# A fixed order of TensorE's work in the expert loop: first product, next tokens, turn, selection, second product

## The chip, the cores and the metric

The kernel runs on one NeuronCore of a Trainium2 chip. Its time is the device time of one execution in microseconds (us); before and after are compared by the median of several executions. One execution of each kernel is also profiled, and the rows below come from that one.

## The reference

Two transformer blocks over 512 tokens of width 1024, in float32. The first block has a mixer (a gated delta rule beside sliding-window attention) and then a mixture of experts; the second block has two feed-forward layers around another mixer. The change lies in the mixture of experts:

```python
out = jnp.zeros(t.shape, jnp.float32)
for e in range(N_EXPERTS):                               # 32 experts
    hid = jax.nn.silu(t @ w_gate[e]) * (t @ w_up[e])     # 1024 -> 2 x 256
    out = out + combine[:, e:e + 1] * (hid @ w_down[e])  # 256 -> 1024
```

`combine` is zero but for the two experts that a token has chosen, so each expert needs only its own tokens: 32 of the 512 on the mean.

## The kernel before, in words

The kernel is one program for the five engines, written with a library that records the operations, places their buffers and then puts each engine's instructions in an order of its own, by readiness and priority under its model of times; data dependences become semaphores. So the order of the source isn't the order on an engine.

The experts are worked through in `moe` in 8 quads of 4 experts. A quad's first pass takes at most 32 tokens of each expert: the array's 128 columns are split in four strips of 32, and four matmuls, one per expert, run side by side. In quad q:

- `expert1` (line 1257), the **first product**: 8 steps of the inner dimension times 4 experts, 32 matmuls of 512 columns on the gate and up weights. The profile records a float32 matmul as two, so 64 records. ScalarE and VectorE then make the gated units `mth` from it (lines 1247 to 1249: tanh, scalar-tensor-tensor, product).
- `xpose` (line 1228): 8 **token transposes** of `xg`, the gathered tokens of quad q+1; `feed` scales them into `xgT`, VectorE the even and ScalarE the odd ones (lines 1218, 1216). `xgT` has one buffer, which the running first product still reads.
- `turn` (line 1266): two transposes of `mth`, copied by ScalarE into `hT` (line 1268).
- `expert2` (line 1289), the **second product**: 16 matmuls of 512 columns on the down weights; ScalarE scales the result into `ys` (line 1290), GpSimd scatters it.
- `gather(q + 2)` with `select` (line 1173): the **selection**, 32 small matmuls as recorded, of 3 columns, gives the token numbers of the quad after the next; GpSimd then gathers these tokens.
- `more`, per expert: under a condition read from the data (line 1347) a **wide pass** over up to 128 more tokens. In these data one expert of each quad takes it. Behind each `more`, six weight tiles of 512 KB are asked for (`load`, line 1031, by SyncE's queue).
- `ahead(q + 1)` (lines 1340, 1342): under conditions again, the selection for the next wide pass (line 1203).

What stands under a condition can't move out of it, nor the rest in. So between `ahead(q)` and `more` the library is free in the order of the first product, token transposes, turn, second product and selection; that is the stretch that the change touches. The weights have 31 buffers: 24 tiles of a quad and 7 of the next.

Of the kernel before, what the change touches and what calls it, by code (L numbers as in the profile page):

```python
# [21 lines left out]
KT = 8  # L22
# [182 lines left out]
class Net:  # L205
# [804 lines left out]
    def moe(self):  # L1010


        nc, v, s, g_, pe = self.nc, self.nc.vector, self.nc.scalar, self.nc.gpsimd, self.nc.tensor
        A, tc, mp = self.A, self.tc, self.mp
        mm, ident, ones, mod = pe.matmul, self.ident, self.ones, self.mod

        NQ = NE // 4
        first, wide = 32, 128

        def ex(q, c):  # L1020

            return 8 * c + q
# [10 lines left out]
        def piece(w, k):  # L1033

            return w[k // 2][:, k % 2 * S:k % 2 * S + S]
# [17 lines left out]
        for i in range(4):  # L1053
            for hf in range(2):
                pt = self.pst([P, S], "mm")
# [6 lines left out]
        def sm(shape, tag):  # L1062
            return self.t(mp, shape, "r_" + tag)
# [79 lines left out]
        val = sm([P, 4, NE, 3], "val")  # L1143
# [19 lines left out]
        def select(q):  # L1163

            oh = self.t(mp, [P, 4, 4, first], "oh")
            for i in range(4):
                v.tensor_tensor(oh[:, i], iota[:, :first].unsqueeze(1).to_broadcast([P, 4, first]),
                                rank[:, i, q::8].unsqueeze(2).to_broadcast([P, 4, first]), ALU.is_equal)
            pv = self.pst([P, 3], "mm")
            for i in range(4):  # L1170
                for c in range(4):
                    cs = slice(32 * c, 32 * c + 32)
                    mm(pv[cs, :], oh[:, i, c, :], val[:, i, ex(q, c), :], start=i == 0, stop=i == 3, tile_position=(0, 32 * c))
            if q < NQ - 1:
                idx = self.t(mp, [P, 1], "idy", U32, bufs=4)
                v.tensor_scalar_add(idx, pv[:, 2:3], BIG - 1.0)
            else:
                idx = self.t(mp, [P, 1], "idx")
                v.tensor_scalar_add(idx, pv[:, 0:1], BIG)
            wv = self.t(mp, [P, 1], "wv", bufs=4)  # L1180
            v.tensor_copy(wv, pv[:, 1:2])
            return oh, idx, wv, pv

        def fetch_tokens(xg, idu):
            g_.indirect_dma_start(out=xg, out_offset=None, in_=h2d, in_offset=bass.IndirectOffsetOnAxis(ap=idu, axis=0),
                                  bounds_check=S - 1, oob_is_err=False)

        def gather(q):

            _, idx, wv, pv = select(q)  # L1190
            idu = self.t(mp, [P, 1], "idu", U32, bufs=4)
            v.tensor_scalar_add(idu, pv[:, 0:1], BIG - 1.0)
            fetch_tokens(xg, idu[:, 0:1])
            return xg, idx, wv
# [25 lines left out]
        def xtiles():  # L1220
            return [self.t(mp, [P, 4, P], f"xgT{hf}") for hf in range(2)]

        def xpose(xg, xTs=None):
            xTs = xTs or xtiles()
            for hf in range(2):
                pt = self.pst([P, 4, P], "mm")
                for k in range(4):
                    pe.transpose(pt[:, k, :], xg[:, (4 * hf + k) * P:(4 * hf + k + 1) * P], ident)
                feed(xTs, hf, pt)
            return xTs  # L1230
# [14 lines left out]
        def glu(th, gate, up):  # L1245

            s.activation(th, gate, AF.Tanh, scale=0.5)
            v.scalar_tensor_tensor(th, th, 1.0, gate, op0=ALU.add, op1=ALU.mult)
            v.tensor_mul(th, th, up)

        def expert1(q, xT):
            ps = self.pst([P, 2, 2, P], "mm")
            ws = [[wt[ex(q, c), j] for j in range(4)] for c in range(4)]
            for k in range(KT):
                for c in range(4):
                    cs = slice(32 * c, 32 * c + 32)
                    mm(ps[cs].rearrange("p a b c -> p (a b c)"), xT[k // 4][:, k % 4, cs], piece(ws[c], k),  # L1257
                       start=k == 0, stop=k == KT - 1, tile_position=(0, 32 * c))
            th = self.t(mp, [P, 2, P], "mth")
            glu(th, ps[:, :, 0, :], ps[:, :, 1, :])  # L1260
            return th

        def turn(th):
            pt = self.pst([P, 2, P], "mm")
            for k in range(2):
                pe.transpose(pt[:, k, :], th[:, k, :], ident)
            hT = self.t(mp, [P, 2, P], "hT")
            s.copy(hT, pt)
            return hT
# [5 lines left out]
        def expert2(q, hT, idx, wv):  # L1275

            late = q == NQ - 1
            ys = yt[:1]
            if late:
                ys = [self.t(mp, [P, D], f"ys{i}", F32R) for i in range(2)]  # L1280
                ys.append(self.t(self.tp, [P, S], "sq", F32R))
                v.tensor_scalar(ys[-1], tokens, idx, None, op0=ALU.is_equal)
            for n in range(2):
                py = self.pst([P, S], "mm")
                ns = slice(n * S, (n + 1) * S)
                for k in range(2):
                    for c in range(4):
                        cs = slice(32 * c, 32 * c + 32)
                        mm(py[cs, :], hT[:, k, cs], wt[ex(q, c), 4 + k][:, ns], start=k == 0, stop=k == 1, tile_position=(0, 32 * c))  # L1289
                s.activation(ys[0][:, ns], py, AF.Copy, scale=wv)  # L1290
                if late:
                    v.scalar_tensor_tensor(ys[1][:, ns], py, wv, ys[0][:, ns], op0=ALU.mult, op1=ALU.subtract)
            if not late:
                scatter(ys[0], idx[:, 0:1])
            return ys
# [41 lines left out]
        def ahead(q):  # L1337

            for h in range(2):
                with tc.If(rvs[NE + 8 * h + q] > first):  # L1340
                    for c in (2 * h, 2 * h + 1):
                        with tc.If(rvs[ex(q, c)] > first):
                            gather_wide(ex(q, c), 1)
# [37 lines left out]
        gat = {0: select(0)}  # L1381
        xt = pick(gat[0][0])
        gat[1] = gather(1)
        count(0)
        for q in range(NQ):
            last = q == NQ - 1
            th = expert1(q, xt)
            if q == 0:
                ahead(0)
            if not last:  # L1390
                xt = xpose(gat[q + 1][0])
                count(q + 1)
            hT = turn(th)
            if not last:
                expert2(q, hT, *gat[q][1:3])
                if q + 2 < NQ:
                    gat[q + 2] = gather(q + 2)
            for c in range(4):
                more(ex(q, c))
                load(6)  # L1400
            if not last:
                ahead(q + 1)
# [518 lines left out]
```

## Time and profile before

| what | value |
|---|---|
| median of 3 runs | 2187.48 us (2181.98 to 2188.98) |
| profiled execution | 2189.56 us, span of the trace 2187.7 us |
| TensorE busy | 2028.8 us, 93% of the span |
| first products, line 1257 | 512 records, 77.7 us |
| second products, line 1289 | 256 records, 49.5 us |
| expert loop, first product of quad 0 to the scatter of quad 7 | 497.3 to 804.4 us |

The trace gives for each instruction its start and length, and for the idle time of an engine before it what ended it. A view by stretches gives busy time per engine and the TensorE clock granted, as a share of 2.4 GHz: 1.00 is the full clock, 0.50 is 1.2 GHz.

### The profile page before, as it was taken

Reading aid. Unit: us, or ns where it says so; the run is one execution under the profiler, and the core shown is the slowest. Engines: PE = TensorE matmul, PEld = TensorE weight load, DVE = VectorE, ACT = ScalarE, POOL = GpSimd, SP = SyncE. Lnnn points to the kernel's source line nnn. Section 1 sums busy time; section 2 is a strip of 40 time slices with the busy share of each in tenths; the row PEclk is TensorE's granted clock in tenths of the full one; section 3 lists DMA queues with packets and bytes.
Section 4 is the critical chain, followed back from the end, with each engine's and each line's share of the span. In section 5 each row is a group of like instructions: output and inputs, shape, how many; then the busy total and the mean of one; then the engine's idle time right before and its main releaser. Section 6 shows DMA issues by size and latency. Waiting matters only on the chain.

```text
span 2187.7 us, 32948 instructions
## 1 busy us (share of the span) xinstructions
PE 2028.8 (93%) x13074; PEld 1566.6 (72%) x13074; DVE 1045.1 (48%) x1947; ACT 703.9 (32%) x1173; POOL 186.2 (9%) x208
## 2 busy tenths in 40 slices
PE   5999999788888878999999899999999999999996
PEld 3677767554343438888888788888878888888886
DVE  4663564742111127552354764745564447542454
ACT  3432343121221214322233342534452343322231
POOL 3020002001001012000002300000000031000002
PEclk9999999888898989999999999999999999999998
DMA  7343315057999854233232232323222322233321
GB/s 266 107 127 104 101 55 177 30 181 306 383 347 352 333 216 142 97 93 99 100 97 94 72 92 70 123 63 113 64 98 93 109 78 81 98 90 98 106 87 40
DMA packets 106470, 294.40 MB, mean 135 GB/s; under 512 B 16087, under 2 KB 27351, under 8 KB 106284
## 3 DMA queue, kind: packets, MB, share of 16 engines
q1 hardware_dynamic: 99676, 275.98, 36.7%
q0 software_dynamic: 6032, 13.85, 1.9%
q8 instruction: 117, 1.92, 0.4%
q10 hardware_dynamic: 576, 2.10, 0.2%
q14 instruction: 69, 0.57, 0.1%
HBM read 283.53 MB, written 18.13 MB: 138 GB/s over the span
## 4 chain that ended last, share of the span: by engine, by line
PE 56%; DVE 3%; POOL 1%; ACT 1%; issue 1%; DMA 0%; POOLq 0%; SPq 0%; ACTq 0%; DVEq 0%
PE mm L274 18%; PE mm L273 18%; PE mm L275 17%; DVE xl L1535 1%; PE sm L1633 1%; POOL x L1487 1%; PE mm L1661 1%; DVE cy L1486 1%; PE mm L1658 0%; DVE wl L257 0%; PE sm L1648 0%; PE sm L1787 0%; POOL ss L339 0%; ACT wh L256 0%; DVE rs_a L297 0%
## 5 line engine op out<-in xcount | busy, mean ns | idle before, releaser
L273 PE MATMUL mm<-xh,wh 128*128 128x512 f32 (+1 forms) x1584 | 615.3, 391 | 5.6 <-ACT xh L1534 4.1
L274 PE MATMUL mm<-xl,wh 128*128 128x512 f32 (+1 forms) x1584 | 606.0, 383 | 4.9 <-DVE xl L1535 4.9
L275 PE MATMUL mm<-xh,wl 128*128 128x512 f32 (+1 forms) x1584 | 603.4, 382 | 0.5 <-DVE wl L257 0.5
L256 ACT ACTIVATE wh<-wraw 128x1024 fp32r<-128x1024 f32 (+3 forms) x282 | 274.2, 974 | 747.6 <-PE mm L274 663.6
L257 DVE TENSOR_TENSOR wl<-wraw,wh 128x1024 fp32r<-128x1024 f32 (+3 forms) x282 | 314.6, 1116 | 192.1 <-ACT wh L256 190.4
L273 PEld LDWEIGHTS mm<-xh,wh 128*128 128x128 f32 x1584 | 301.9, 192 | 71.8 <-issue 8.3
L274 PEld LDWEIGHTS mm<-xl,wh 128*128 128x128 f32 x1584 | 303.2, 191 | 60.8 <-DVE xl L1535 6.6
L275 PEld LDWEIGHTS mm<-xh,wl 128*128 128x128 f32 x1584 | 302.3, 191 | 57.1 <-issue 1.2
L273 PE MATMUL mm<-hh,wh 128*128 128x512 f32 (+1 forms) x416 | 148.5, 357 | 0.0
L275 PE MATMUL mm<-hh,wl 128*128 128x512 f32 (+1 forms) x416 | 148.3, 357 | 0.0
L274 PE MATMUL mm<-hl,wh 128*128 128x512 f32 (+1 forms) x416 | 148.2, 356 | 0.0
L339 POOL TENSOR_TENSOR ss<-ss,sq 128x256 f32<-128x256 f32 (+1 forms) x69 | 65.7, 952 | 915.9 <-ACT sq L338 913.4
L275 PEld LDWEIGHTS mm<-hh,wl 128*128 128x128 f32 x416 | 78.6, 189 | 11.3
L273 PEld LDWEIGHTS mm<-hh,wh 128*128 128x128 f32 x416 | 78.6, 189 | 11.3
L274 PEld LDWEIGHTS mm<-hl,wh 128*128 128x128 f32 x416 | 78.6, 189 | 11.2
L1257 PE MATMUL mm<-wmoe,xgT 128*32 128x512 f32 x512 | 77.7, 630 | 6.8 <-PEq L1340 4.9
L1595 DVE TENSOR_TENSOR sq<-mm,rsb 128x512 f32<-128x512 f32 x44 | 30.4, 691 | 104.0 <-PE mm L275 103.8
L1590 DVE TENSOR_TENSOR cy<-mm,rsb 128x512 f32<-128x512 f32 x44 | 30.4, 691 | 85.4 <-PE mm L275 83.5
L1289 PE MATMUL mm<-wmoe,hT 128*32 128x512 f32 x256 | 49.5, 742 | 9.5 <-PEq L1405 6.3
L1218 DVE TENSOR_SCALAR xgT<-mm,gs,mod 128x128 f32<-128x128 f32 x32 | 13.1, 409 | 80.4 <-PE mm L1257 66.5
L1257 PEld LDWEIGHTS mm<-wmoe,xgT 128*32 128x32 f32 x512 | 18.2, 114 | 45.6 <-issue 43.4
L1216 ACT ACTIVATE xgT<-mm,mod,gs 128x128 f32<-128x128 f32 x32 | 14.6, 459 | 107.1 <-DVE xgT L1218 98.8
(496 smaller groups left out, 2600.6 us busy)
## 6 DMA issues: line engine op xcount, KB each, us to landing
wmoe<-in_wmoe SPq DMA_DIRECT2D x192, 512.0 KB
wraw<-in_win SPq DMA_DIRECT2D x90, 512.0 KB
wraw<-in_wgu SPq DMA_DIRECT2D x88, 512.0 KB
wraw<-in_wada SPq DMA_DIRECT2D x32, 512.0 KB
wraw<-in_wd SPq DMA_DIRECT2D x32, 448.0 KB
big<-in_wada SPq DMA_DIRECT2D x16, 512.0 KB
wraw<-in_wd SPq DMA_DIRECT2D x16, 512.0 KB
wraw<-in_wout SPq DMA_DIRECT2D x16, 256.0 KB
```

Source lines behind the costliest of these rows:

```text
L256: self.nc.scalar.activation(h[:, :n], raw[:, :n], AF.Copy)
L257: self.nc.vector.tensor_sub(l[:, :n], raw[:, :n], h[:, :n])
L273: mm(ps, w1, xh[k], start=start and i == 0, stop=False)
L274: mm(ps, w1, xl[k], start=False, stop=False)
L275: mm(ps, w2, xh[k], start=False, stop=stop and i == nk - 1)
L339: self.nc.gpsimd.tensor_add(acc[:, hs], acc[:, hs], sq[:, hs])
L1257: mm(ps[cs].rearrange("p a b c -> p (a b c)"), xT[k // 4][:, k % 4, cs], piece(ws[c], k), start=k == 0, stop=k == KT - 1, tile_position=(0 ...
L1289: mm(py[cs, :], hT[:, k, cs], wt[ex(q, c), 4 + k][:, ns], start=k == 0, stop=k == 1, tile_position=(0, 32 * c))
L1486: self.nc.vector.scalar_tensor_tensor(t[:, hs], f[k][:, hs], gcol[:, k:k + 1], pb, op0=ALU.mult, op1=ALU.mult)
L1487: (self.nc.gpsimd if k % 2 else self.nc.vector).tensor_add(self.x[k][:, hs], self.x[k][:, hs], t[:, hs])
L1590: v.tensor_mul(t1, pp[0], rb)
L1595: v.tensor_mul(t2, pp[1], rb)
```

## The change

Nothing is added or taken away. Four blocks of recorded instructions are bound to stand behind an instruction of the same engine: token transposes and turn behind the last matmul of the first product, the selection behind the turn, the second product behind the selection (in quad 6, which has none, behind the turn). `issue_after` binds only the instructions on that instruction's engine, here TensorE; the other engines' orders follow from the library's planning. The source now also records the selection ahead of the second product.

```diff
-                    mm(pv[cs, :], oh[:, i, c, :], val[:, i, ex(q, c), :], start=i == 0, stop=i == 3, tile_position=(0, 32 * c))
+                    self.chosen = mm(pv[cs, :], oh[:, i, c, :], val[:, i, ex(q, c), :], start=i == 0, stop=i == 3, tile_position=(0, 32 * c))
...
-                    mm(ps[cs].rearrange("p a b c -> p (a b c)"), xT[k // 4][:, k % 4, cs], piece(ws[c], k),
-                       start=k == 0, stop=k == KT - 1, tile_position=(0, 32 * c))
+                    self.end1 = mm(ps[cs].rearrange("p a b c -> p (a b c)"), xT[k // 4][:, k % 4, cs], piece(ws[c], k),
+                                   start=k == 0, stop=k == KT - 1, tile_position=(0, 32 * c))
...
-                pe.transpose(pt[:, k, :], th[:, k, :], ident)
+                self.turned = pe.transpose(pt[:, k, :], th[:, k, :], ident)
...
             if not last:
-                xt = xpose(gat[q + 1][0])
+                with tc.issue_after(self.end1.ins):
+                    xt = xpose(gat[q + 1][0])
                 count(q + 1)
-            hT = turn(th)
+            with tc.issue_after(self.end1.ins):
+                hT = turn(th)
             if not last:
-                expert2(q, hT, *gat[q][1:3])
                 if q + 2 < NQ:
-                    gat[q + 2] = gather(q + 2)
+                    with tc.issue_after(self.turned.ins):
+                        gat[q + 2] = gather(q + 2)
+                with tc.issue_after((self.chosen if q + 2 < NQ else self.turned).ins):
+                    expert2(q, hT, *gat[q][1:3])
```

TensorE at the start of quad 2, before. `mm_6253` is the first product's sum, `xg` the tokens of quad 3, `mm_6292` and `mm_6301` their transposes; the four `wmoe` are the first weight tiles of the four experts.

```order
L1340 UNCONDITIONAL_BRANCH
L1257 MATMUL mm_6253<-wmoe_5583,xgT_938_5748 32x512
L1228 MATMUL mm_6292<-c_ident_64,xg_4714 128x128 x2
L1257 MATMUL mm_6253<-wmoe_5651,xgT_938_5748 32x512
L1228 MATMUL mm_6292<-c_ident_64,xg_4714 128x128 x2
L1228 MATMUL mm_6301<-c_ident_64,xg_4714 128x128 x4
L1257 MATMUL mm_6253<-wmoe_5973,xgT_938_5748 32x512
L1257 MATMUL mm_6253<-wmoe_5981,xgT_938_5748 32x512
```

The same place now:

```order
L1340 UNCONDITIONAL_BRANCH
L1257 MATMUL mm_6253<-wmoe_5583,xgT_938_5748 32x512
L1257 MATMUL mm_6253<-wmoe_5651,xgT_938_5748 32x512
L1257 MATMUL mm_6253<-wmoe_5973,xgT_938_5748 32x512
L1257 MATMUL mm_6253<-wmoe_5981,xgT_938_5748 32x512
```

The transposes have left the start of the first product; quads 1 and 3 to 6 differ in the same way. In quad 0 they stood behind it already.

TensorE at the end of the first product of quad 2, before: the turn of `mth`, six matmuls of the second product (sums `mm_6399` and `mm_6409`), the selection, the other ten.

```order
L1257 MATMUL mm_6253<-wmoe_6047,xgT_939_5749 32x512
L1266 MATMUL mm_6394<-c_ident_64,mth_6286 128x128 x2
L1289 MATMUL mm_6399<-wmoe_6049,hT_6397 32x512
L1289 MATMUL mm_6399<-wmoe_6053,hT_6397 32x512
L1289 MATMUL mm_6409<-wmoe_6049,hT_6397 32x512
L1289 MATMUL mm_6399<-wmoe_6117,hT_6397 32x512
L1289 MATMUL mm_6409<-wmoe_6053,hT_6397 32x512
L1289 MATMUL mm_6409<-wmoe_6117,hT_6397 32x512
L1173 MATMUL mm_6427<-r_val_4875,oh_6422 32x3 x16
L1289 MATMUL mm_6399<-wmoe_6121,hT_6397 32x512
```

The same place now (the sums of the second product are `mm_6430` and `mm_6440`):

```order
L1257 MATMUL mm_6253<-wmoe_6047,xgT_939_5749 32x512
L1228 MATMUL mm_6292<-c_ident_64,xg_4714 128x128 x4
L1228 MATMUL mm_6301<-c_ident_64,xg_4714 128x128 x4
L1266 MATMUL mm_6394<-c_ident_64,mth_6286 128x128 x2
L1173 MATMUL mm_6404<-r_val_4875,oh_6399 32x3 x16
L1289 MATMUL mm_6430<-wmoe_6049,hT_6397 32x512
L1289 MATMUL mm_6430<-wmoe_6053,hT_6397 32x512
L1289 MATMUL mm_6440<-wmoe_6049,hT_6397 32x512
```

Token transposes stand ahead of the turn and the selection ahead of all of the second product, whose own order is as before. Quads 1 to 5 are alike. In quad 0 the selection stood behind the second product and now stands ahead of it; quad 6 has no selection; quad 7 is as it was.

VectorE around the gated units `mth` of quad 2, before:

```order
L1218 TENSOR_SCALAR xgT_1013_6290<-mm_6292,gs_663_4410,mod_104 128x128 x2
L1218 TENSOR_SCALAR xgT_1014_6291<-mm_6301,gs_663_4410,mod_104 128x128
L1248 SCALAR_TENSOR_TENSOR mth_6286<-mth_6286,mm_6253 128x256
L1249 TENSOR_TENSOR mth_6286<-mth_6286,mm_6253 128x256
L1218 TENSOR_SCALAR xgT_1014_6291<-mm_6301,gs_663_4410,mod_104 128x128
L1176 TENSOR_SCALAR idy_6444<-mm_6427 128x1
```

and now:

```order
L1248 SCALAR_TENSOR_TENSOR mth_6286<-mth_6286,mm_6253 128x256
L1218 TENSOR_SCALAR xgT_1013_6290<-mm_6292,gs_663_4410,mod_104 128x128
L1249 TENSOR_TENSOR mth_6286<-mth_6286,mm_6253 128x256
L1218 TENSOR_SCALAR xgT_1014_6291<-mm_6301,gs_663_4410,mod_104 128x128
L1218 TENSOR_SCALAR xgT_1013_6290<-mm_6292,gs_663_4410,mod_104 128x128
L1176 TENSOR_SCALAR idy_6421<-mm_6404 128x1
```

One scaling of the next tokens now stands between the two steps that make `mth`, where three stood ahead of them.

## Rows read from the trace of the kernel before

**Rows 1.** Stretches (us): five engines' busy time with instructions, clock, DMA share, GB/s; quad 2's whole period.
```profile
578.91:619.56 40.65, 33.50 (x197) 15.53 (x198) 7.26 (x25) 8.11 (x18) 4.06 (x4) 0.88 0.91 351
```
**Rows 2.** Stretches, quads 1 to 6: start of the first product to end of the second.
```profile
537.97:560.23 22.26, 20.41 (x138) 6.78 (x138) 3.48 (x13) 3.17 (x7) 2.05 (x2) 0.82 1.02 415
578.91:600.70 21.79, 19.93 (x138) 5.66 (x138) 3.49 (x13) 3.17 (x7) 2.05 (x2) 0.82 0.86 343
...
660.88:682.64 21.76, 19.90 (x138) 5.60 (x138) 3.48 (x13) 3.17 (x7) 2.05 (x2) 0.82 0.80 317
701.80:721.00 19.20, 17.25 (x138) 5.59 (x138) 3.08 (x10) 3.17 (x7) 2.05 (x2) 0.88 0.90 356
740.49:758.88 18.39, 16.44 (x106) 5.38 (x106) 2.39 (x6) 2.49 (x6) 1.03 (x1) 0.81 0.87 352
```
**Rows 3.** Timeline (start, length, engine, line, operation, idle before), TensorE in quad 2.
```profile
578.91 1.88 PE L1257 MATMUL mm<-wmoe,xgT 128*32 128x512 f32 x2 [0.41 <-DMA wmoe<-in_wmoe]
580.72 0.69 PE L1228 MATMUL mm<-c_ident,xg 128*128 128x128 f32 x2
...
583.19 0.99 PE L1228 MATMUL mm<-c_ident,xg 128*128 128x128 f32 x6
584.11 7.06 PE L1257 MATMUL mm<-wmoe,xgT 128*32 128x512 f32 x60
592.57 0.44 PE L1266 MATMUL mm<-c_ident,mth 128*128 128x128 f32 x2 [1.40 <-DVE mth L1249]
593.47 2.60 PE L1289 MATMUL mm<-wmoe,hT 128*32 128x512 f32 x9 [0.46 <-ACT hT L1268]
...
596.68 0.59 PE L1173 MATMUL mm<-r_val,oh 128*32 128x3 f32 x29
...
597.12 3.57 PE L1289 MATMUL mm<-wmoe,hT 128*32 128x512 f32 x19
```
**Rows 4.** Stretches: first product of quads 2 and 7, first product's end to second's end, quads 2, 5.
```profile
578.91:591.17 12.26, 12.26 (x72) 3.33 (x72) 0.82 (x2) 0.91 (x2) 1.03 (x1) 0.81 1.03 414
591.17:600.70 9.53, 7.67 (x66) 2.33 (x66) 2.67 (x11) 2.26 (x5) 1.01 (x1) 0.82 0.65 251
...
712.99:721.00 8.01, 6.06 (x66) 1.97 (x66) 2.26 (x8) 2.26 (x5) 1.02 (x1) 1.00 0.71 274
...
778.66:787.09 8.43, 8.43 (x64) 2.37 (x64) 0.00 (x0) 0.00 (x0) 1.04 (x1) 0.83 0.81 324
```
**Rows 5.** Timeline, TensorE: second product and selection of quad 0.
```profile
513.97 4.22 PE L1289 MATMUL mm<-wmoe,hT 128*32 128x512 f32 x32 [0.46 <-ACT hT L1268]
518.02 0.45 PE L1173 MATMUL mm<-r_val,oh 128*32 128x3 f32 x32
```
**Rows 6.** Timeline, ScalarE and VectorE between the products of quad 2.
```profile
591.22 0.38 ACT L1247 ACTIVATE mth<-mm 128x256 f32<-128x256 f32 x1 [1.53 <-PE mm L1257]
591.22 0.41 DVE L1218 TENSOR_SCALAR xgT<-mm,gs,mod 128x128 f32<-128x128 f32 x1 [2.02 <-PE mm L1257]
591.63 0.42 DVE L1248 SCALAR_TENSOR_TENSOR mth<-mth,mm 128x256 f32<-128x256 f32 x1
...
592.09 0.42 DVE L1249 TENSOR_TENSOR mth<-mth,mm 128x256 f32<-128x256 f32 x1
```
**Rows 7.** Timeline, TensorE's weight loads (PEld) in quad 1.
```profile
543.12 0.16 PEld L1257 LDWEIGHTS mm<-wmoe,xgT 128*32 128x32 f32 x8 [1.22 <-DMA wmoe<-in_wmoe]
```
**Rows 8.** Timeline, TensorE: start of the wide pass of quad 0.
```profile
519.82 1.06 PE L1228 MATMUL mm<-c_ident,htok 128*128 128x128 f32 x8 [1.34 <-DVEq L1347]
```
**Rows 9.** Timeline, TensorE: transposes behind the expert loop.
```profile
818.03 1.09 PE L1375 MATMUL mm<-c_ident,wmoe 128*128 128x128 f32 x8 [1.07 <-DVE x L1329]
820.57 1.09 PE L1375 MATMUL mm<-c_ident,wmoe 128*128 128x128 f32 x8 [1.45 <-POOL wmoe L1371]
```
**Rows 10.** Stretch with these transposes.
```profile
816.96:821.42 4.46, 1.94 (x17) 1.71 (x17) 3.72 (x13) 0.00 (x0) 4.08 (x3) 1.00 1.02 419
```
**Rows 11.** Timeline, GpSimd: the gather behind the selection of quad 2.
```profile
598.41 1.01 POOL L1185 DMA_INDIRECT xg<-h2d,idu  x1 [18.42 <-DVE idu L1192]
```

## The prediction

> **What bounds the kernel now.** I read the stretches by quad first, then TensorE's timeline in one quad, then what ended its idle time, then the DMA. In the expert loop a quad repeats every 41 us: quad 2 takes 40.65 us, in which TensorE is busy 33.50 us and the DMA moves 351 GB/s at a share of 0.91 [rows 1]. The 24 weight tiles of a quad are 24 x 524,288 bytes = 12.6 MB; at the 415 GB/s of quad 1 [rows 2] that is 30.3 us. So from quad 2 on the transfers have about 10 us to spare in each period, and they wait for TensorE to free buffers. VectorE and ScalarE are busy 7.26 and 8.11 us of 40.65. What sets the pace is the chain through TensorE: first product, gated units, turn, second product, then the conditions and the wide pass. The change touches only the stretch from the start of the first product to the end of the second: 21.79 us in quad 2, 21.76 in quad 4 (quad 3 lies within 0.2 us of these), 22.26 in quad 1, 19.20 in quad 5 and 18.39 in quad 6 [rows 2].
>
> In this stretch the reader is to see three losses [rows 3]. (1) At 578.91 a lone matmul of the first product runs (2 records, 1.88 us), then two transposes, then another lone one, then six transposes; only at 584.11 do the four strips run together, and 60 of the 64 records take 7.06 us. Four experts side by side cost no more than one, so a lone matmul pays the price of four. (2) From 591.17 to 593.47 TensorE does nothing but the turn: 1.40 us idle for `mth`, 0.46 us for `hT`. (3) The second product starts at 593.47 and ends at 600.69, with the selection in its midst: 12 records, then the selection, then 20 more that alone take 3.6 us, because the last records run one strip after another.
>
> The clock adds to it. It stands at 0.81 over the first product [rows 4], which starts at half clock behind the quiet end of the quad before. Over the stretch from first product's end to the second's it is 0.82 in quad 2 and 1.00 in quad 5, which takes 8.01 us there instead of 9.53 [rows 4]: in quad 2 the clock fell to 1.2 GHz when the second product began, behind the 1.9 us of idleness, and in quad 5, with the same order, it didn't.
>
> **First product, made contiguous.** Quad 7 shows it before the change, since no tokens follow: 64 records in 8.43 us at clock 0.83 [rows 4], which is 8.43 x 0.83 = 7.0 us of full-clock work. Quad 2 has a half-clock part of 2 x (1 - 0.81) x 12.26 = 4.7 us; with it the same work takes 7.0 + 4.7 / 2 = 9.35 us. So the bounds for quads 2 to 6 are 8.43 and 9.35 us, depending on where the clock rises; I take 8.9.
>
> **From the first product's end to the second's.** The 8 transposes move here: 1.06 us at full clock by a like group of 8 [rows 8]. They need only PE and lie in the 1.40 us that wait for `mth`. But their first scaling now stands on VectorE between the two steps that make `mth`. Before, tanh (0.38 us) and one scaling (0.41) ran side by side, then came 0.42 and 0.42 [rows 6]; now it is tanh, 0.42, 0.41, 0.42. So the turn comes 0.41 to 0.45 us later, at 1.40 + 0.45 = 1.85 us behind the first product. Then 0.44 us of turn [rows 3] and the selection, 0.45 us [rows 5], which now covers the 0.46 us wait for `hT`. The second product starts at 1.85 + 0.44 + 0.45 = 2.75 us. Alone it takes 4.22 us in quad 0, the first two groups of four records still at half clock; at full clock 8 groups of four at 0.43 us (7.06 us over 15 groups, less the last one's 0.6 us, [rows 3]) and a tail of 0.17 make 3.6 us. Sum at full clock: 2.75 + 3.6 = 6.35 us, against 9.53 in quad 2 and 8.01 in quad 5. If the clock falls as it does now (quad 2's 9.53 us at 0.82 hold 2 x 0.18 x 9.53 = 3.4 us at half), it takes 1.7 us more: 8.05.
>
> Does it fall? Of the stretch that preceded the fall, 1.9 us were idle; now only 0.75 + 0.05 us are. I take the full clock, 6.35 us, and keep 8.05 as the other end. What the trace shows of transposes bears on it: behind the loop TensorE ran 16 of them and little else from 816.96 to 821.42, with waits of 1.07 and 1.45 us between [rows 9], and the clock stayed at 1.00 [rows 10].
>
> The Trainium skill says otherwise (TensorE: Matmul & The Clock Gate, section Part 4: PE-mode transpose): a transpose doesn't count as busy the way a matmul does, and the full clock doesn't engage for it. By that rule the filled gap is as quiet as it was; that is the second rival below; the stretch of [rows 10] speaks against it.
>
> **Quads 2 to 6.** Each 8.9 + 6.35 = 15.25 us (quad 6 has no selection, but `hT` then sets the same start). Before: 3 x 21.8 + 19.2 + 18.4 = 103.0. After: 76.3. Gain 26.7 us; with all at 9.35 it is 24.5, with all at 8.43 it is 29.1.
>
> **Quad 1** gains less. Its weights come late, since quad 0's wide pass holds its buffers: a weight load waits for a transfer until 543.12, 5.15 us after the first product began [rows 2, 7], and the transposes that filled this time now stand behind. Three experts' first matmuls run, then TensorE idles some 3 us, and starts again at half clock: 5.15 + 7.0 + 1.7 = 13.85 us for the first product, then 6.35. That is 20.2 against the 22.26 us of now [rows 2]: gain 2.0 us, between -1 (clock low in both products and no part of the wait used) and 4 (no new idle time).
>
> **Quad 0** gains the selection that moves into the `hT` wait, 0.2 us, and of the 1.34 us in which the wide pass waits for VectorE, which worked off the late selection [rows 8], what the other quads don't have: they wait 0.64 us or less at that place, so 0.7. Together 0.9 us, between 0 and 1.3. Quad 7 and what lies behind gain nothing.
>
> What hides the rest: the gathers and scatters on GpSimd keep their order; the gather is issued 1.1 us after the selection (598.41, [rows 11]) and its tokens are wanted at the end of the next first product, later in the quad than now. A third scaling on VectorE and three on ScalarE move behind the turn and end beside the second product; should they not be done at its end, the wide pass would wait, up to 0.9 us a quad. SP's queue has 24 issues in the same order. With 41 - 5.5 = 35 us a quad, 30.3 us of transfers still fit.
>
> **Sum.** 26.7 + 2.0 + 0.9 = 29.6 us off the profiled execution's 2189.56: 2160. That one lies 2.1 us above the median of the runs, 2187.48; the same off the median, rounded, gives 2158.
>
> **Rivals.**
> 1. Forecast, 66%: 2158; its own range, by 8.43 or 9.35 us and quad 1's bounds, 2152 to 2166.
> 2. The clock still falls before every second product, 15%: 6 quads x 1.7 = 10.2 us dearer, 2168. For: the rule above; the gap has 0.8 us of idleness left and the selection's matmuls have 3 columns. Against: [rows 9, 10], and quad 5, which kept its clock with 8.01 - 6.06 = 1.95 us idle [rows 4].
> 3. The weights become the bound, 9%: as in quad 1, a first product that starts sooner meets late tiles. A 3 us stall with 1.5 us of half clock behind it in 5 quads costs 22 us: 2180. For: the DMA's share of 0.91. Against: its 10 us to spare.
> 4. The order isn't the limit and the period stays at 41 us, 6%: 2187. For: the four periods from quad 1's start to quad 5's are 40.7 to 41.3 us by their starts [rows 1, 2], though quad 1 waited for weights and the others did not. Against: quad 5's shorter stretch shortened its period to 38.7 us (701.80 to 740.49, [rows 2]).
> 5. Slower, 4%: the transposes stand ahead of turn, selection and second product, and TensorE works in order; if the gathered tokens are late, all of it waits. The gather is issued some 2.5 us before a quad's end; conditions, wide pass (18.9 us, 600.70 to 619.56) and first product (8.9) follow, so its tokens have 30 us. A landing 35 us after the issue would eat the gain of 5.3 us a quad; at 38 us every one of six quads is 3 us longer than now: 2205. For: nothing was ordered behind this landing so tightly. Against: the transposes at the start of a quad come some 21 us after the gather's issue (598.41 [rows 11], quad 3 at 619.56 [rows 1]), and in quad 2 no wait stands before them [rows 3].
>
> **How the numbers follow.** What can be told from no change is 0.3%, 6.6 us: below 2181 is faster, above 2194 slower. Cases 1, 2 and two thirds of 3 lie below 2181: 87%. The rest of 3 and 4: 9% the same. 4% slower. The range: from 2147 (case 1 with 8.43 us everywhere, quad 1 at its best and 3 us of scatter among runs) to 2178 (case 2 and part of 3).
>
> **What would show it.** After: 64 records of the first product in one row of 8.4 to 9.4 us in quads 2 to 6, 16 second-product matmuls in one row of about 3.6 us at clock 1.00, 6.3 to 6.5 us between the ends of the two products, quads of about 35 us, and quad 1 with an idle gap of 3 us in its first product. Rows of 5.3 us for the second product mean rival 2; DMA as what ends TensorE's idle time in quads 2 to 6 means rival 3; the gather as that means rival 5. Wrong in kind is the forecast if the two products shrink and the period of 41 us doesn't.

## The result, and the profile after

The changed kernel takes 2158.7 us (median of 4 runs, 2156.94 to 2161.09); before, in the same rounds, 2188.23 us (2181.98 to 2196.13). The ratio is 0.9864, 95% interval [0.983, 0.9898]: faster by 29.5 us. Its profiled execution has a span of 2155.1 us, 32.6 less than before's.

A view by stretches, for quads 1 to 6 from the start of the first product to the end of the second, and the whole period of quad 2 last. Columns: stretch, its length, busy time (instructions) of TensorE, its weight loads, VectorE, ScalarE, GpSimd, then granted clock, DMA share, GB/s.

```profile
536.11:555.49 19.38, 17.77 (x138) 5.01 (x138) 3.16 (x13) 3.07 (x7) 1.97 (x2) 0.85 1.03 413
574.09:589.90 15.81, 15.12 (x138) 5.14 (x138) 3.16 (x13) 2.38 (x6) 2.08 (x2) 0.84 1.03 416
608.79:624.31 15.52, 14.84 (x138) 5.02 (x138) 3.16 (x13) 2.38 (x6) 2.07 (x2) 0.85 1.02 409
643.79:658.99 15.20, 14.52 (x138) 6.82 (x138) 3.16 (x13) 2.38 (x6) 2.08 (x2) 0.88 1.02 412
678.03:693.14 15.11, 14.33 (x138) 4.97 (x138) 2.75 (x10) 2.38 (x6) 2.06 (x2) 0.88 1.02 404
713.02:727.73 14.71, 13.56 (x106) 4.64 (x106) 2.16 (x6) 2.39 (x6) 1.04 (x1) 0.90 1.02 402
574.09:608.79 34.70, 29.16 (x196) 15.37 (x197) 6.90 (x25) 7.83 (x18) 4.09 (x4) 0.89 1.02 412
```

Against [rows 2] quads 2 to 6 are 6.0, 6.4, 6.6, 4.1 and 3.7 us shorter, quad 1 by 2.9. (Quad 3 of before, not among those rows, took 21.9 us.) Quad 2's period fell from 40.65 us [rows 1] to 34.70; the five of quads 2 to 6 are 34.7, 35.0, 34.2, 35.0 and 34.2 us. From the end of a second product to the next first product nothing moved: 18.6 to 19.9 us, before 18.7 to 19.8. The DMA's share rose from 0.91 to 1.02.

TensorE's timeline in quad 2 (start, length, line, operation, idle time before), to be laid beside [rows 3]:

```profile
574.09 9.63 PE L1257 MATMUL mm<-wmoe,xgT 128*32 128x512 f32 x64 [0.84 <-PEq L1340]
583.65 1.09 PE L1228 MATMUL mm<-c_ident,xg 128*128 128x128 f32 x8
585.33 0.44 PE L1266 MATMUL mm<-c_ident,mth 128*128 128x128 f32 x2 [0.59 <-DVE mth L1249]
585.70 0.43 PE L1173 MATMUL mm<-r_val,oh 128*32 128x3 f32 x32
586.23 3.67 PE L1289 MATMUL mm<-wmoe,hT 128*32 128x512 f32 x32
```

One row each for the first product, the selection and the second product, where before had several. The 1.40 us of waiting for `mth` are 1.09 us of transposes and 0.59 us of waiting; the wait for `hT` is gone under the selection.

The two halves of quad 2, for comparison with the first two of [rows 4]:

```profile
574.09:583.72 9.63, 9.63 (x65) 2.73 (x66) 0.00 (x0) 0.00 (x0) 1.04 (x1) 0.73 1.03 413
583.72:589.90 6.18, 5.49 (x74) 2.42 (x74) 3.16 (x13) 2.38 (x6) 1.04 (x1) 1.00 1.03 420
```

The first product is 2.63 us shorter though its mean clock is lower (0.73 for 0.81): the half-clock part, 2 x 0.27 x 9.63 = 5.2 us, is a larger share of less work. The second half runs at the full clock, 6.18 us for 9.53; in quads 3 to 6 it takes 6.17 to 6.27 us.

Quad 1, TensorE's timeline, and one row of its weight loads (PEld):

```profile
536.11 1.93 PE L1257 MATMUL mm<-wmoe,xgT 128*32 128x512 f32 x6 [1.19 <-PEq L1340]
538.84 8.48 PE L1257 MATMUL mm<-wmoe,xgT 128*32 128x512 f32 x58 [0.80 <-DMA wmoe<-in_wmoe]
...
549.80 5.69 PE L1289 MATMUL mm<-wmoe,hT 128*32 128x512 f32 x32
```

```profile
551.87 0.16 PEld L1289 LDWEIGHTS mm<-wmoe,hT 128*32 128x32 f32 x8 [1.06 <-DMA wmoe<-in_wmoe]
```

Here both products wait for weights: three experts start, TensorE idles 0.80 us, and the second product takes 5.69 us at clock 1.00 (547.32 to 555.49), 2.0 more than in quad 2: a weight load in it stands still 1.06 us for a transfer, and behind it the loads of the strips come one by one.

By stretches the 32.6 us of span come from the first products of quads 2 to 6, 13.5 us; from what follows them there, 13.3; from quad 1, 2.9; from quad 0, 1.0; and some 2 us from ahead of and behind the loop, where nothing was changed.

### The profile page after: what moved, and what is told of

Read it like the earlier page. It is cut to its first block, busy times and chain, and to the rows that moved or that the text cites. A ratio compares the mean times of both kernels' runs of the same rounds, so it can differ in the third digit from the quotient of the medians.

```text
span 2155.1 us, 32955 instructions
## 1 busy us (share of the span) xinstructions
PE 2000.7 (93%) x13074; PEld 1559.6 (72%) x13074; DVE 1042.6 (48%) x1947; ACT 702.7 (33%) x1173; POOL 186.4 (9%) x208
## 5 line engine op out<-in xcount | busy, mean ns | idle before, releaser
L275 PEld LDWEIGHTS mm<-hh,wl 128*128 128x128 f32 x416 | 78.6, 189 | 11.1
L1257 PE MATMUL mm<-wmoe,xgT 128*32 128x512 f32 x512 | 72.1, 706 | 7.8 <-DMA wmoe<-in_wmoe 3.7
L1786 DVE TENSOR_TENSOR f<-mm,rsb 128x512 f32<-128x512 f32 x24 | 16.4, 688 | 52.1 <-PE mm L275 51.2
L1289 PE MATMUL mm<-wmoe,hT 128*32 128x512 f32 x256 | 33.6, 636 | 7.4 <-PEq L1410 6.3
```

Of the source, the lines that this page charges most:

```text
L275: mm(ps, w2, xh[k], start=False, stop=stop and i == nk - 1)
L1257: self.end1 = mm(ps[cs].rearrange("p a b c -> p (a b c)"), xT[k // 4][:, k % 4, cs], piece(ws[c], k), start=k == 0, stop=k == KT - 1, tile ...
L1786: v.tensor_mul(dst, ps, rb)
```

## The experiments

**The first half of the change alone.** Transposes and turn stay bound behind the first product; selection and second product are free again.

```diff
             if not last:
+                expert2(q, hT, *gat[q][1:3])
                 if q + 2 < NQ:
-                    with tc.issue_after(self.turned.ins):
-                        gat[q + 2] = gather(q + 2)
-                with tc.issue_after((self.chosen if q + 2 < NQ else self.turned).ins):
-                    expert2(q, hT, *gat[q][1:3])
+                    gat[q + 2] = gather(q + 2)
```

> The change's first half alone: token transposes and turn stand behind the first product, the selection is free and stands in the midst of the second product, as before. Theory (the parts add up; the filled gap keeps the clock full, the selection splits the strips): first products as short as in the changed kernel, 8.4 to 9.7 us in quads 2 to 6; clock 1.00 from the first product's end to the second's, and 1.61 + 0.44 + 0.46 + 5.65 = 8.15 us there in quads 2 to 5 instead of 6.2, and about 1 us more in quad 0: 2158.7 + 10.8 = about 2169.5. Rival (the selection's place keeps the clock, not the transposes): the clock falls in four quads as before, 1.7 us each: about 2176.

Measured: 2171.12 us (2167.3 to 2173.71), ratio 0.9928 [0.9912, 0.9945]. The selection is in the second product's midst again. Quad 2, TensorE's timeline and the stretch from the first product's end:

```profile
588.81 1.49 PE L1289 MATMUL mm<-wmoe,hT 128*32 128x512 f32 x9 [0.46 <-ACT hT L1268]
589.71 0.23 PE L1173 MATMUL mm<-r_val,oh 128*32 128x3 f32 x2
590.12 0.61 PE L1289 MATMUL mm<-wmoe,hT 128*32 128x512 f32 x3
590.55 0.44 PE L1173 MATMUL mm<-r_val,oh 128*32 128x3 f32 x29
...
590.83 3.63 PE L1289 MATMUL mm<-wmoe,hT 128*32 128x512 f32 x19
```

```profile
586.30:594.46 8.16, 7.12 (x74) 2.75 (x74) 3.25 (x13) 3.07 (x7) 1.01 (x1) 1.00 0.99 404
```

At the full clock the second product takes 5.65 us with the selection in it (588.81 to 594.46; the same in quads 1 to 5) and 3.67 behind it. So an interleaved selection costs 2.0 us a quad with no help from the clock. The theory held: the clock did not fall, and the time is 1.6 us above its 2169.5.

**The second half alone.** Selection ahead of the second product as in the change; transposes and turn are free.

```diff
-                with tc.issue_after(self.end1.ins):
-                    xt = xpose(gat[q + 1][0])
+                xt = xpose(gat[q + 1][0])
                 count(q + 1)
-            with tc.issue_after(self.end1.ins):
-                hT = turn(th)
+            hT = turn(th)
```

> The change's second half alone: selection ahead of the second product, token transposes free and standing in the first product, as before. Theory (the gap is empty again, so the clock falls when the second product starts): first products as before, 10.7 to 12.4 us in quads 2 to 6 (13.5 us in sum over the changed kernel), second product in one piece but at half clock, 1.40 + 0.44 + 0.45 + 3.67 + 1.7 = 7.7 us between the products' ends: 2158.7 + 13.5 + 7.3 = about 2180. Rival (transposes have nothing to do with the clock): 6.0 us between the ends, about 2171.

Measured: 2176.27 us (2175.89 to 2178.05), ratio 0.9956 [0.9939, 0.9972], between the two. The reason is the clock. From the first product's end to the second's, in quads 2 and 3:

```profile
584.90:592.57 7.67, 6.18 (x68) 2.07 (x66) 2.67 (x11) 1.57 (x4) 1.01 (x1) 0.78 0.84 339
623.61:629.57 5.96, 4.47 (x66) 1.63 (x66) 2.67 (x11) 1.58 (x4) 1.01 (x1) 1.00 0.84 320
```

The order is the same in both, the wait for `mth` too (1.40 us idle). In quads 2, 4 and 5 the clock fell in the second product and it took 5.4 us; in quads 1, 3 and 6 it did not, and in 3 and 6 it took 3.67. A fall costs 7.67 - 5.96 = 1.71 us here. The two halves alone save 15.7 and 9.6 us by their ratios (0.0072 and 0.0044 of 2187), 25.3 together; the whole change saves 29.7. The intervals of the three are too wide to call the 4 us between them an interplay.

**The gap left empty.** The transposes and scalings of the next tokens are left out from quad 1 on, so that later quads multiply the tokens of quad 1; turn, selection and second product keep the changed order.

```diff
-                with tc.issue_after(self.end1.ins):
-                    xt = xpose(gat[q + 1][0])
+                if q == 0:
+                    with tc.issue_after(self.end1.ins):
+                        xt = xpose(gat[q + 1][0])
```

> The changed kernel without the token transposes and their scalings from quad 1 on (the later quads work on the tokens of quad 1), so TensorE has nothing to do while the gated units are made. Theory (the transposes in the gap keep the clock full): the turn comes 0.2 us sooner, but the clock falls to 0.50 in the second product and takes 1.7 us: 2158.7 + 6 x 1.5 = about 2168. Rival (transposes don't count for the clock; it stayed full because the selection covers the wait for hT): the clock stays at 1.00 and the time is 2158.7 - 1.2 = about 2157.5.

Measured: 2162.18 us (2159.57 to 2162.58), ratio 0.9885 [0.9868, 0.9901]. The time alone lies between the two, the trace does not. TensorE's timeline behind the first product of quad 2, and the stretches from the first product's end to the second's in quads 1 and 2:

```profile
587.82 0.41 PE L1266 MATMUL mm<-c_ident,mth 128*128 128x128 f32 x2 [1.50 <-DVE mth L1249]
588.15 0.43 PE L1173 MATMUL mm<-r_val,oh 128*32 128x3 f32 x32
588.75 3.67 PE L1289 MATMUL mm<-wmoe,hT 128*32 128x512 f32 x32 [0.16 <-ACT hT L1268]
```

```profile
551.07:559.11 8.04, 6.41 (x66) 2.38 (x66) 1.93 (x9) 0.95 (x3) 1.01 (x1) 0.79 1.03 419
586.32:592.42 6.10, 4.44 (x66) 1.63 (x66) 1.94 (x9) 0.76 (x2) 1.01 (x1) 1.00 1.02 418
```

With 1.50 us of idle time in place of the transposes the clock stayed at 1.00 in the second products of quads 2 to 6, and in quads 2 to 4 the stretch is as long as in the changed kernel (in quads 5 and 6 the second product took 4.7 and 5.0 us, at clock 1.00 too). So in these quads the transposes in the gap are not what holds the clock. It fell in quad 1 alone, where the first product waited for weights and took 13.35 us, and there the transposes may matter: with the first half of the change alone, quad 1's first product was as long, 13.34 us, also with a wait for weights, but the gap behind it was filled, and the clock stayed:

```profile
549.77:557.91 8.14, 7.12 (x75) 2.75 (x74) 3.25 (x13) 3.07 (x7) 1.02 (x1) 1.00 1.03 420
```

In the loop, from quad 0's first product to quad 7's, the kernel with the empty gap needs 251.7 us and the changed one 250.8. Of the 5.7 us between their profiled spans 4.8 lie ahead of this stretch and behind it, and the intervals of the two ratios overlap.

**Half of the first product.** Four of its eight steps of the inner dimension are left out; all weights are still loaded.

```diff
-            for k in range(KT):
+            for k in range(KT // 2):
...
-                                   start=k == 0, stop=k == KT - 1, tile_position=(0, 32 * c))
+                                   start=k == 0, stop=k == KT // 2 - 1, tile_position=(0, 32 * c))
```

> The changed kernel with half of the first product left out (4 of the 8 steps of the inner dimension); all weights are still loaded. Theory A (TensorE's chain still sets the period): 3.4 to 4.3 us less in each of 7 quads, period about 31 us, time about 2131. Theory B (the DMA does now: 13.8 MB in a period of 34.6 us is 400 GB/s, near the 415 that it reaches): the period can't fall under 13.8 / 0.415 = 33.3 us, weights end TensorE's idle time in quads 2 to 7, and the time is 2150 or more.

Measured: 2157.42 us (2154.32 to 2160.73), ratio 0.9872 [0.9855, 0.9888]: half of a 9 us product gone in eight quads, and the time is that of the changed kernel. The five periods of quads 2 to 6, and what TensorE waited for from 560 to 750 us (total, times, longest):

```profile
572.16:745.08 172.92, 138.82 (x788) 72.66 (x789) 33.25 (x115) 39.98 (x90) 18.98 (x19) 0.90 1.01 398
```

```profile
PE mm L1257 <- DMA wmoe<-in_wmoe: 3.8, 3, 1.7
...
PE mm L1289 <- DMA wmoe<-in_wmoe: 2.9, 5, 0.6
```

The first products of quads 2 to 6 shrank to 5.3 to 6.6 us, and the second products grew from 3.67 to 5.1 to 8.6 us at clock 1.00, waiting for weights tile by tile. With the product halved the bound is the DMA: it moves 68.8 MB in the five periods, 13.8 MB a quad at 398 GB/s and a share of 1.01, and a period takes 34.6 us. The changed kernel's five take no longer, 173.1 us for 69.1 MB.

**A sixth of the weights left out**, the counterpart: the sixth tile of each expert is not loaded.

```diff
-        todo = iter([(ex(q, c), j) for q in range(NQ) for js in (range(4), range(4, 6)) for c in range(4) for j in js])
+        todo = iter([(ex(q, c), j) for q in range(NQ) for js in (range(4), range(4, 5)) for c in range(4) for j in js])
...
+                if j == 4:
+                    wt[e, 5] = w
...
-                load(6)
+                load(5)
```

> The changed kernel with a sixth of the expert weights left out: the sixth tile of each expert is never loaded, the fifth stands in for it, so that a quad asks for 20 tiles of 512 KB and not 24 (11.7 MB and not 13.8 with the gathered tokens and results: 28 us at 415 GB/s and not 33). All other work stays. Theory (in the changed kernel TensorE's chain and the transfers are both at 34 to 35 us per quad): quad 1 falls from 38 to about 35 us, quads 2 to 6 by less than 1 us each, some 2152 to 2156 us. Rival (the transfers alone are the bound since the change): quads 2 to 6 fall to 30 to 32 us, by 3 us each and more: 2135 to 2142 us.

Measured: 2156.82 us (2153.9 to 2158.87), ratio 0.985 [0.9832, 0.9868]. The second quad's period and all five periods of quads 2 to 6, then the same five of the changed kernel:

```profile
572.32:606.82 34.50, 28.89 (x196) 15.06 (x197) 6.93 (x25) 8.00 (x18) 4.08 (x4) 0.90 0.95 363
572.32:743.95 171.63, 143.27 (x949) 77.43 (x950) 33.24 (x115) 40.00 (x90) 19.30 (x19) 0.90 0.90 337
```

```profile
574.09:747.21 173.12, 141.94 (x949) 77.23 (x949) 33.06 (x115) 39.17 (x90) 19.35 (x19) 0.90 1.01 399
```

Quad 1 fell from 38.0 to 34.7 us, the other five from 173.1 to 171.6 us together, 0.3 each, with the DMA at a share of 0.90. So TensorE's own chain is 34.3 us long, and the transfers take 34.6, as the halved product showed. Relieving either alone leaves the period where it is. The theory of two equal bounds held, though the time is 0.8 us above its range, and the one of the transfers alone fell.

**Lone matmuls, in a fixed order.** In quads 1 to 6 the first eight matmuls of the first product and the eight transposes take turns. Of the edit, the part that sets the order (`one()` issues one matmul of the first product, `pts` receives the transposes of the next tokens `nxt`):

```diff
...
+                    if prior is None:
+                        self.end1 = one()
+                    else:
+                        with tc.issue_after(prior.ins):
+                            self.end1 = one()
+                    if pts is not None and n < 8:
+                        with tc.issue_after(self.end1.ins):
+                            prior = pe.transpose(pts[n // 4][:, n % 4, :], nxt[:, n * P:(n + 1) * P], ident)
+                        n += 1
...
```

> The changed kernel, but in quads 1 to 6 the first eight matmuls of the first product and the eight transposes of the next tokens take turns one by one, in a fixed order; all the rest, selection and second product included, as in the changed kernel. Theory (what the change gives at the first product's start is the four strips running side by side: a strip matmul with a transpose on either side runs alone, and alone one costs what four cost together): before shows two records alone at 1.88 us at the half clock (0.95 us at the full one), where four matmuls together take about 1.05 us. Eight lone matmuls in place of two groups of four then cost 8 x (0.95 to 1.9) - 2 x 1.05 = 5.5 to 13 us more per quad, less the 1.1 us of transposes behind the product, in six quads 26 to 72 us: 2185 to 2231 us, 2210 for about half of each stretch at the half clock. Rival (only the switching between the two kinds of work costs, strips alone or together alike): at most 0.2 us per switch, 16 switches, in part hidden since the transfers leave no room: 2159 to 2170 us.

Measured: 2206.13 us (2204.21 to 2209.1), ratio 1.0073 [1.0056, 1.009], slower than before. TensorE's timeline in quad 2:

```profile
583.28 1.88 PE L1262 MATMUL mm<-wmoe,xgT 128*32 128x512 f32 x2 [0.41 <-DVE oix L1208]
585.10 0.48 PE L1272 MATMUL mm<-c_ident,xg 128*128 128x128 f32 x1
585.50 1.79 PE L1262 MATMUL mm<-wmoe,xgT 128*32 128x512 f32 x2
587.22 0.33 PE L1272 MATMUL mm<-c_ident,xg 128*128 128x128 f32 x1
587.48 1.04 PE L1262 MATMUL mm<-wmoe,xgT 128*32 128x512 f32 x2
588.46 0.33 PE L1272 MATMUL mm<-c_ident,xg 128*128 128x128 f32 x1
...
594.90 5.36 PE L1262 MATMUL mm<-wmoe,xgT 128*32 128x512 f32 x48
```

At the full clock a lone matmul (2 records) takes 1.04 us. The last 48 records are 24 matmuls, six groups of four, in 5.36 us: 0.89 us for four. The theory held, and the switching, 0.07 us of overlap at each border, costs nothing visible. The Trainium skill (TensorE: Matmul & The Clock Gate, section Part 3: Packing small matmuls — row/col tiling) says that matmuls on different strips run at the same time; the 0.89 us for four beside 1.04 us for one agree with it, and add that one transpose between two of them ends it.

**VectorE's scalings behind the gated units.**

```diff
-            v.tensor_mul(th, th, up)
+            self.gated = v.tensor_mul(th, th, up)
...
-                with tc.issue_after(self.end1.ins):
+                with tc.issue_after(self.end1.ins), tc.issue_after(self.gated.ins):
                     xt = xpose(gat[q + 1][0])
```

> The changed kernel, but VectorE's scalings of the next tokens (its half of them) stand behind the last step of the gated units on VectorE; ScalarE's half as before. Theory (TensorE's wait of 0.59 us ahead of the turn is the wait for the gated units, and the scalings put between their steps on VectorE make none of it): the turn stays at 1.6 us behind the first product's end and the time at 2158 to 2160 us. Rival (the scalings delay the gated units by 0.2 us): the turn comes at 1.4 us in six quads, and the time falls by at most 1.2 us, 2157 us.

Measured: 2160.64 us (2156.13 to 2164.47), ratio 0.9867 [0.9845, 0.9888]. VectorE behind the first product of quad 2, in the changed kernel and then in this one:

```profile
584.20 0.42 DVE L1248 SCALAR_TENSOR_TENSOR mth<-mth,mm 128x256 f32<-128x256 f32 x1 [10.63 <-ACT mth L1247]
584.54 0.41 DVE L1218 TENSOR_SCALAR xgT<-mm,gs,mod 128x128 f32<-128x128 f32 x1
584.86 0.41 DVE L1249 TENSOR_TENSOR mth<-mth,mm 128x256 f32<-128x256 f32 x1
```

```profile
583.47 0.42 DVE L1248 SCALAR_TENSOR_TENSOR mth<-mth,mm 128x256 f32<-128x256 f32 x1 [10.56 <-ACT mth L1247]
583.93 0.42 DVE L1249 TENSOR_TENSOR mth<-mth,mm 128x256 f32<-128x256 f32 x1
```

The scaling between the two steps costs 0.66 - 0.46 = 0.20 us from start to start, not its own 0.41. Without it the turn comes at 1.41 us behind the product, the wait for `mth` is 0.39 us; a new wait of 0.16 us for `hT` leaves 0.14 us of the gain. The rival is right on the mechanism; 0.14 us in six quads can't be seen in the time.

**SyncE's reads behind its weight requests.** Why did quad 1 get its weights late? SyncE's queue in quad 0 of the changed kernel: weight requests up to 506.07 us, then this group of reads of the token counts (durations in ns, first and last start in us), and the next request at 526.74.

```profile
L1335 SPq TENSOR_LOAD <-r_cmi x30: 262/267/531, 506.5 to 524.7; - x30
```

```profile
514.00:520.00 6.00, 5.36 (x44) 2.43 (x37) 1.84 (x6) 2.73 (x5) 2.06 (x2) 0.96 0.46 163
520.00:526.00 6.00, 6.00 (x30) 5.23 (x29) 0.99 (x3) 1.45 (x4) 0.00 (x0) 1.00 0.15 56
```

The 30 reads serve five quads; the library had put them all into quad 0. The DMA's share fell to 0.15. Before the change it was the same: requests up to 508.13 us, then these reads, and the next request at 530.83.

```profile
L1335 SPq TENSOR_LOAD <-r_cmi x34: 86/264/555, 508.5 to 528.8; - x34
```

```diff
-                nc.sync.dma_start(w, A["wmoe"][e, :, 1024 * j:1024 * j + 1024])
+                self.loaded = nc.sync.dma_start(w, A["wmoe"][e, :, 1024 * j:1024 * j + 1024])
...
-                count(q + 1)
+                with tc.issue_after(self.loaded.ins):
+                    count(q + 1)
```

> The changed kernel, with one more order: on every queue's engine that asks for weights (SyncE), reading the counts of quad q+1 stands behind the last weight request of quad q-1. In the changed kernel SyncE reads the counts of five quads in a row in quad 0, about 30 reads of 0.55 us from 506.5 to 525.3 us, and asks for no weights in that time; the transfers' share falls to 0.46 and 0.15 in 514 to 526 us, and quad 1 waits for weights in both products. Theory (those reads cost quad 1 its weights): the requests go out some 9 us earlier, quad 1 loses its waits (0.8 us, and 2.0 us of its second product's 5.7) and falls from 38.0 to about 35 us; later quads stay at 34 to 35, since TensorE's own chain there (14.7 to 15.8 and 18.6 to 19.9 us) is as long: about 2155 us. Rival (buffers, not the queue, hold the weights back in quad 0, since a tile's buffer comes free only when its expert is done): no change, 2158 to 2160 us. Third case (transfers alone set all later quads): all 7 to 9 us come through, 2150 us.

Measured: 2154.72 us (2153.14 to 2162.1), ratio 0.9839 [0.9825, 0.9853]. Quad 1 took 34.96 us, its products 9.84 and 3.67, with no wait for weights; quads 2 to 6 stayed at 34.1 to 35.0. As the changed kernel had been timed in other rounds, both ran once more side by side.

> The changed kernel once more, on the same chip and in the same rounds as the next one, so that the two can be compared. Both theories: 2157 to 2160 us, quad 1 at 38 us.

> The changed kernel with the reading of the counts behind the weight requests, once more beside the changed kernel. Theory (its quad 1 took 35.0 us in place of 38.0, and nothing else moved): 3 us below the changed kernel of this call, 2155 us. Rival (the 4 us between their medians were the difference of two calls; the profiled run of this kernel gave back in quad 7 and behind it what quad 1 won): the same time as the changed kernel within 0.1%.

Measured: the changed kernel 2161.44 us (2157.85 to 2162.76), 1.4 above what was expected, ratio 0.9889 [0.9871, 0.9907]; with the reads moved 2154.79 us (2153.45 to 2159.57), ratio 0.9855 [0.9837, 0.9872]. By these the second is 0.9966 of the first, plus or minus 0.0025 (the two half-widths of 0.0018 added as squares): 7 us, between 2 and 13. Of the second, quad 1's stretch, SyncE's reads in quads 0 and 1, and the DMA in quad 0:

```profile
538.41:554.32 15.91, 15.22 (x138) 5.10 (x138) 3.15 (x13) 2.38 (x6) 1.75 (x2) 0.83 1.02 409
```

```profile
L1335 SPq TENSOR_LOAD <-r_cmi x18: 262/265/469, 508.8 to 550.3; - x18
```

```profile
518.00:524.00 6.00, 5.25 (x37) 3.52 (x30) 1.64 (x4) 3.04 (x6) 1.02 (x1) 1.00 0.73 210
```

Weight requests go on at 519.6 us, quad 1's stretch is 4.0 us shorter than the 19.95 of the changed kernel beside it, its period 34.84 us for 38.61. The five quads behind it took 174.7 us, for 173.0 in the changed kernel, so that the loop kept 1.9 of the 3.8 us won in quad 1; in the first measurement it kept 3.1. By the medians this version is faster than both kernels. The traces show the mechanism and not the whole 7 us: in both measurements the profiled execution was the slowest of its runs, and its loop began 4 to 5 us later than the changed kernel's.

## Why the prediction came true, and where its steps did not

The forecast was 2158 us; 2158.7 were measured.

**The sum.** Quads 2 to 6 were to take 76.3 us in the changed stretch and took 76.35; with quad 1 (forecast 20.2, measured 19.4) and quad 0 (0.9 and 1.0) the three terms give 30.6 us where 29.6 were forecast. That the sum of quads 2 to 6 fits to 0.1 us is luck in part: two of its terms were off in opposite directions, the first products by 0.8 us and what follows them by 0.7. That the medians agree with the forecast to 1 us is luck as well: the interval of their ratio allows a gain of 22 to 37 us, and the profiled spans differ by 32.6, some 2 of it from outside the loop. For quad 0 one reading was off: the wide passes of the other quads wait 0.53 to 0.83 us, not 0.64 or less; the 0.7 us taken from it fit, since quad 0's wait fell from 1.34 to 0.57.

**First product, 8.9 us.** Measured 9.63, 9.35, 9.03, 8.86, 8.44, mean 9.06. Quad 2 lies above the upper bound of 9.35. The bound took its half-clock part, 4.7 us, from before; it now holds 5.2 us, and 7.0 + 5.2 / 2 = 9.6. The mechanism, that strips lose their neighbours to the transposes, is shown by the lone matmuls (1.04 us for one, 0.89 for four).

**First product's end to second's, 6.35 us.** Measured 6.17 to 6.27. The turn came at 1.61 us, not 1.85: a scaling between two dependent steps was priced at its 0.42 us, and costs 0.20, since VectorE starts independent instructions 0.33 us apart and these two 0.46 us apart. Second product 3.67 us for 3.6. The second product gains from both causes named: 2.0 us from the selection (first half alone, at clock 1.00) and 1.7 us where the clock fell (second half alone).

**The clock.** It stayed full in all second products of quads 1 to 6, as forecast. But the reason that the forecast gave, less idle time ahead of it, isn't shown: with 1.50 us empty the clock stayed up in five quads, and with 1.40 us empty and the transposes in the first product it fell in three of six. In the traces of all kernels here, nine second products of quads 1 to 6 lost the clock. All nine stood behind an empty gap (9 of 24; none of 48 behind a gap with transposes) and behind a first product of 10.4 to 13.4 us, stretched by transposes or by a wait for weights. Behind those of up to 10.0 us the clock stayed with the gap empty or filled; behind those of 11.1 to 13.4 us with a filled gap it stayed in five of five; it stayed too behind the 17 to 18 us with lone matmuls, with an empty gap. So in quads 2 to 6 the shorter first product was enough, whatever stood in the gap; that the transposes hold the clock behind a long one is likely but not shown, and what the clock hangs on stays open.

The Trainium skill's rule (TensorE: Matmul & The Clock Gate, section Part 4: PE-mode transpose) that transposes don't count as busy isn't settled by this: in quads 2 to 6 the clock stayed at 1.00 with or without them, and the two runs of quad 1 set side by side above, 0.79 with an empty gap and 1.00 with a filled one, speak against it.

**Quad 1.** An idle gap of 3 us was forecast; 0.80 us came, and 1.89 in the second trace of the same kernel, since the tile landed 2.7 and 3.8 us behind the start instead of 5.15 (SyncE's queue was free for requests at 526.7 us for 530.8 before). That the second product would wait for weights too, 2.0 us, was not foreseen. The cause named, buffers that the wide pass holds, was wrong for the most part: with the reads on SyncE's queue moved behind the requests, both waits went, with the same buffers, and the trace of before shows the same reads in quad 0.

**Room for the transfers.** "From quad 2 on the transfers have about 10 us to spare in each period" is the step that failed. It counted the weights alone, 12.6 MB at quad 1's 415 GB/s, 30.3 us. All transfers are 13.8 MB a quad, and they take 34.6 us where they set the period (half of the first product). The room was 41 - 34.6 = 6 us, and the change used it to the last: half a first product less brought nothing after it. Rival 3, put aside with these 10 us, was near: TensorE waited for weights once ahead of a first product of quads 2 to 6, 1.00 us in quad 4.

**The rivals.** Rival 2's price of 1.7 us a quad was right (1.71), its event didn't come. Rivals 4 and 5 left no trace: periods fell with the stretch, and no wait for the gathered tokens stands among TensorE's in the five quads.

## What to carry to other kernels

Where four small matmuls share the array, count the places at which something stands between them: each lone one costs what the four cost, and work that fits into a wait a few microseconds later is nearly free there (behind the eight transposes the turn came 0.2 us later). Before such a gain is summed over a loop, set all bytes of an iteration, not the weights alone, against the loop's own rate: the gain ends where the transfers begin to bind. And look at what else stands on the queue that asks for the weights, and in which order: 18 us of register reads ahead of the requests made a quad wait for its weights.

## What the hardware showed that was not expected

- The two bounds of the loop met within half a microsecond, 34.3 us of TensorE's chain and 34.6 us of transfers, so that relieving either one alone moved the time by less than its scatter.
- SyncE reads a count in 0.27 us, but with the arithmetic behind it one took 0.6 us: 30 of them held the queue from 506.5 to 525.3 us, and the DMA fell to 56 GB/s.
- On VectorE an instruction put between two dependent ones cost half its own duration (0.20 of 0.41 us).
